# A 32×32 triangular inverse by columns in place, its steps spread over an RWKV-7 recurrence

## The chip, the core and the metric

The kernel runs on one core of one Trainium2 chip. A core has a matrix engine (TensorE, PE in the rows), three engines that work elementwise on SBUF (VectorE = DVE, ScalarE = ACT, GpSimd = POOL), a queue engine (SyncE = SP) that here issues most loads and stores, and 16 DMA engines. The metric is the device time of one execution in microseconds (us). [...]

## The reference

One inference step of a trunk of two mixing layers, each followed by a gated feed-forward layer: the first mixer is retention beside a gated linear recurrence, the second is RWKV-7. It runs over a prompt of 1024 tokens with 16 learned tokens ahead (1040 columns) and over 8 sample rows with states of their own. All is float32. The change lies in the RWKV-7 mixer:

```
def rwkv7_step(S, inp):
    r_t, w_t, k_t, v_t, a_t, b_t = inp
    sa = jnp.einsum('bhij,bhj->bhi', S, a_t)
    S = S * w_t[:, :, None, :] + sa[..., None] * b_t[:, :, None, :] + v_t[..., None] * k_t[:, :, None, :]
    y = jnp.einsum('bhij,bhj->bhi', S, r_t)
    return S, y
...
    s_new, ys = lax.scan(rwkv7_step, s0.astype(f32), (tm(rh), tm(wh), tm(kh), tm(vh), tm(-kk), tm(kk * ah)))
...
    o = ((ys - mu) * lax.rsqrt(var + GN_EPS_C)).reshape(B, T, D) * p['gn_g'].astype(f32) + p['gn_b'].astype(f32)
    bonus = jnp.sum(rh * kh * p['r_k'].astype(f32), axis=-1, keepdims=True) * vh
    o = (o + bonus.reshape(B, T, D)) * g.astype(f32)
    return o.astype(h.dtype) @ p['w_o'], s_new, h[:, -1], v_first
```

There are 16 heads of 64 channels. The kernel runs the prompt's scan in 17 chunks of 64 tokens (the last has 16). Within a chunk the step-by-step dependence becomes a triangular system (I − A) U = Z per head, with A strictly triangular; its solution takes the inverses of the two 32×32 diagonal blocks and one product for the block below them.

## The kernel before

The RWKV-7 mixer has two parts. `Layer1A` makes the projections r, k and v, each in eight output tiles of 128 features (two heads), over 1040 + 8 columns. A float32 product is three float32r passes on TensorE (`mm`, lines 335 to 337), after ScalarE and VectorE have split each operand in two (323, 324). Beside the products run *side steps*: the table POS gives each a place in sixths of a tile, and `weave` emits it between the eight parts of the tile's products. In the v stage these are, for each tile, the value transposes (`spread` and `tr`: VectorE adds the shift at 1385 and 1388, TensorE transposes at 1401 and 1404), the arithmetic of the 8 sample rows for one head pair (`samp_load`, `samp_pair`, `samp_sum`: loads on SyncE at 1509, elementwise work on VectorE and GpSimd at 1518 to 1530) and two entries of the inverse of block 0. After the last tile `samp_post` forms the sample rows' group norm (`sy` matmuls at 1542 and 1554 and small VectorE instructions at 1543 to 1558). When the tiles are done, `done()` issues the loads of chunk 0's keys (`load_k`), the side steps that are left follow in the order of their places, with `first`, which is `load_v` of chunk 0, among them.

The diagonal blocks are inverted four chunks at a time, one 32×32 block on a partition (4 chunks × 16 heads × 2 = 128 partitions; the fifth group has one chunk and 32 partitions). Such a group is called a block below. `inv_steps` returns a list of steps: `load` (GpSimd's queue: a DMA of the scores `d_ab` to the tile `at`, and memsets of the result `mt` to the unit matrix), `rows` between the given cuts (VectorE, one multiply and one sum for each row t from 1 to 31), and `out` (a transposed copy on VectorE, and two stores on GpSimd's queue to `d_mt` and `d_mm`, from which the chunks' loads on SyncE's queue read at 1680 and 1683).

`Layer1B` runs the recurrence: 17 chunks × 2 halves of the heads = 34 *units*. A unit's pieces are emitted in the order of the string UNIT; the engines run their own instructions in this order, each waiting only for its data. `pa`, `pt`, `p2`, `p3` prepare the next unit (scores `A`, transposes `Tp`, masks to `lz` and `ly` on VectorE), `z`, `u`, `s` and `y` are the chain (the state matmuls `s`, 16 of them, at 1796; the state's scaling on VectorE at 1804; its copies to `s0v` on GpSimd at 1812), `g1` and `g2` are the group norm of the unit before, `o` a part of the output projection of a block of tokens that is complete (from unit 8 on), and `r` takes one step from the list of the inverse, four times a unit. Block j is needed by chunk 4j; `run` makes its list at chunk 4(j − 1), 22 steps and an empty one long, so that in two of eight units the list is empty. Loads of chunk c + 2 are issued at the end of chunk c. 

```
CUTS = [1, 8, 11] + list(range(14, 33))
UNIT = "pa z pt g1 u r r o r p2 g2 o o s o r y p3"
```

Of the kernel before, what the change touches and what calls it, by code (L numbers as in the profile page):

```python
# [8 lines left out]
F32 = mybir.dt.float32  # L9
F32R = mybir.dt.float32r  # L10
AF = mybir.ActivationFunctionType
OP = mybir.AluOpType
# [3 lines left out]
T = 1048  # L16
# [10 lines left out]
NCH = 17  # L27
NTOK = 1040

# ---------------------------------------------------------------- vectors  # L30
# [14 lines left out]
def constants():  # L45
    """Tables that depend on shapes alone."""
# [41 lines left out]
# ---------------------------------------------------------------- host layout  # L88
def cols(v):
    """(..., n*128) -> (128, ..., n): features on partitions."""  # L90
    v = np.asarray(v)
    r = v.reshape(v.shape[:-1] + (v.shape[-1] // 128, 128))
    return np.moveaxis(r, -1, 0)


def wblocks(w):
    """(K, M) -> (M/128, 128, K/128 * 128): one block per 128 output features."""
# [4 lines left out]
def gblocks(w, groups):  # L102
    """(K, 1024) cut along K in groups of g tiles -> blocks that hold 8, 4 or 2 output tiles x g K-tiles."""
# [73 lines left out]
def unlayout(o):  # L177
# [15 lines left out]
# where the parts of a head pair's arithmetic stand beside the next products, in sixths of a 128-wide output tile  # L193
# [5 lines left out]
       0.69, "v.s2": 1.38, "v.sum": 4.97, "v7.pair": 2.3, "v7.post": 5.46, "v7.post_d": 0.5, "v.fold": 1.57, "v.tr0":  # L199
# [3 lines left out]
# K-tiles between stages of which GpSimd takes the lower part  # L203
POOL = (1, 3, 4)

# and of which it takes the mix
MIXP = (4,)

# shares of PE time given to the parts beside the products
L0K = {"start": 0.088, "rope": 0.5, "tr": 1.05, "ret0": 1.312, "ret": 0.35, "lru0": 2.42, "lru1": 2.2, "lru2": 2.2,  # L210
       "lru3": 1.76, "conv": 3.221, "group": 0.748, "wait": 3.6, "norm": 0.845, "norm1": 0.28}
# ---------------------------------------------------------------- device
# [4 lines left out]
class Weave:  # L217
    """Emits dense steps and, between them, side steps as their share of the time comes up."""
# [43 lines left out]
class Prog:  # L262
# [6 lines left out]
    # ---- weights: loads two blocks ahead, exact split into two float32r parts one block ahead  # L269
# [33 lines left out]
    def scale_w(self, t, kind, j):  # L303
        """Scales a block of w1 | a1 (or g1) by mix (j = 0) or 1 - mix along K."""
# [21 lines left out]
    # ---- one PSUM bank of a product: sum over k of W[k]^T X[k], in three exact float32r passes  # L326
# [21 lines left out]
    # steps of one 128-wide output tile, each token block in so many parts; evac(tb, psum view, c0, c1).  # L348
    # late: the weights of the next tile are not split before this one; pre: they are once its products are out
# [18 lines left out]
    # two tiles side by side at the start of a phase, each token block as soon as its norm is there  # L368
# [1716 lines left out]
```

## Time and profile before

| | |
|---|---|
| median of 3 runs | 3529.23 us (3525.82 to 3534.32) |
| profiled execution: span from first to last instruction | 3527.9 us |
| busy in the span: TensorE, VectorE, ScalarE, GpSimd | 94%, 51%, 35%, 10% |
| value stage, 2096 to 2204 us: TensorE, VectorE, GpSimd busy | 92.6, 92.7, 66.5 of 108.0 us |
| recurrence, 2231.4 to 2672.1 us: TensorE, VectorE, GpSimd busy | 366.3, 350.6, 85.6 of 440.7 us |
| granted clock over the whole span | 0.961 |

A row of the trace names an instruction by engine and line of the kernel, with out<-in by the program's names. The busy time of an engine counts its instructions, not its waits; a matmul's end is modelled. The bracket at the end of a row gives the idle time of the engine just before, and what ended it. The profiled execution's span is 1.3 us below the median of the runs. The stages in the middle of the span have different limits, so busy shares are read by stretch and not over the whole.

### The profile page before, as it was taken

How to read it: one execution, taken by the hardware profiler on the slowest of the kernel's cores; microseconds unless marked ns; L12 is line 12 of the kernel's file. 1: busy time of each engine (PE TensorE's matmuls, PEld its weight loads, DVE VectorE, ACT ScalarE, POOL GpSimd, SP SyncE). 2: the span in 40 equal slices, each digit the busy share in tenths (PEclk: the TensorE clock that was granted, in tenths of full speed). 3: DMA queues.
4: the chain of work that ended last, by engine and by line, in shares of the span. 5: the costliest groups of instructions: out<-in, count | busy, mean ns of one | idle time of the engine just before them, and what ended most of it. 6: DMA issues, size and time to landing. Idle time of an engine off the chain costs nothing.

```text
span 3527.9 us, 55814 instructions
## 1 busy us (share of the span) xinstructions
PE 3305.9 (94%) x23480; PEld 3123.5 (89%) x23480; DVE 1800.3 (51%) x2860; ACT 1241.4 (35%) x2214; POOL 361.6 (10%) x650
## 2 busy tenths in 40 slices
PE   8999999998999999998978978788889999999998
PEld 7999999997999999997978878566767999999997
DVE  4444445556433333334765658677885533333334
ACT  4222224555322212123674444344445312212122
POOL 0110110000000000000111236111210000000000
PEclk9999999999999999999999989678999999999999
DMA  4111211111111111111356768845543111111111
GB/s 134 62 56 60 74 40 46 46 47 34 42 43 48 48 48 42 42 53 48 118 169 169 176 172 232 219 119 143 152 129 96 37 49 46 45 49 42 48 48 64
DMA packets 303066, 294.33 MB, mean 83 GB/s; under 512 B 233056, under 2 KB 248704, under 8 KB 300640
## 3 DMA queue, kind: packets, MB, share of 16 engines
q1 hardware_dynamic: 294368, 262.95, 25.6%
q0 software_dynamic: 8448, 27.82, 2.5%
q8 instruction: 185, 3.03, 0.4%
q14 instruction: 65, 0.53, 0.1%
HBM read 218.95 MB, written 67.47 MB: 81 GB/s over the span
## 4 chain that ended last, share of the span: by engine, by line
PE 29%; DVE 12%; DMA 4%; ACT 3%; issue 3%; SPq 1%; POOL 1%; DVEq 0%; POOLq 0%; ACTq 0%
PE d L337 8%; PE d L335 8%; PE d L336 8%; DVE pr L1439 2%; DVE mt L1441 1%; PE hs L1325 1%; DVE xsl L324 1%; DMA x<-d_pp 1%; DVE wl L324 1%; DMA kq<-d_kq 1%; PE nrm L429 1%; DMA at<-d_ab 1%; DVE x L1213 1%; DVE T L1439 0%; ACT x L1188 0%
## 5 line engine op out<-in xcount | busy, mean ns | idle before, releaser
L335 PE MATMUL d<-xsh,wh 128*128 128x350 f32 (+1 forms) x3656 | 1207.6, 330 | 11.5 <-ACT xsh L323 7.7
L337 PE MATMUL d<-xsl,wh 128*128 128x350 f32 (+1 forms) x3656 | 1193.6, 326 | 5.2 <-DVE xsl L324 5.1
L336 PE MATMUL d<-xsh,wl 128*128 128x350 f32 (+1 forms) x3656 | 1188.0, 325 | 4.4 <-DVE wl L324 4.4
L335 PEld LDWEIGHTS d<-xsh,wh 128*128 128x128 f32 x3656 | 696.2, 190 | 23.2 <-ACT xsh L323 9.3
L337 PEld LDWEIGHTS d<-xsl,wh 128*128 128x128 f32 x3656 | 694.6, 190 | 16.0 <-DVE xsl L324 14.7
L336 PEld LDWEIGHTS d<-xsh,wl 128*128 128x128 f32 x3656 | 696.9, 191 | 7.1 <-DVE wl L324 5.2
L335 PE MATMUL d<-T,wh 128*128 128x350 f32 (+1 forms) x1380 | 463.7, 336 | 15.8 <-DVE x L405 8.9
L324 DVE TENSOR_TENSOR wl<-wst,wh 128x1024 fp32r<-128x1024 f32 x248 | 303.1, 1223 | 320.3 <-ACT wh L323 320.3
L336 PE MATMUL d<-T,wl 128*128 128x350 f32 (+1 forms) x1380 | 445.2, 323 | 2.5 <-DVE wl L324 2.5
L337 PE MATMUL d<-T,wh 128*128 128x350 f32 (+1 forms) x1380 | 445.3, 323 | 1.4 <-DVE T L324 1.4
L323 ACT ACTIVATE wh<-wst 128x1024 fp32r<-128x1024 f32 x248 | 260.7, 1051 | 509.2 <-PE d L337 387.8
L405 DVE TENSOR_TENSOR x<-d,x 128x350 f32<-128x350 f32 (+1 forms) x450 | 230.3, 520 | 322.2 <-PE d L337 322.1
L991 DVE SCALAR_TENSOR_TENSOR T<-T,vec 128x1064 f32<-128x1064 f32 x88 | 116.8, 1327 | 398.2 <-ACT T L989 396.6
L335 PEld LDWEIGHTS d<-T,wh 128*128 128x128 f32 x1380 | 260.0, 188 | 28.2 <-DVE x L405 10.2
L336 PEld LDWEIGHTS d<-T,wl 128*128 128x128 f32 x1380 | 260.1, 188 | 9.9 <-DVE wl L324 3.2
L337 PEld LDWEIGHTS d<-T,wh 128*128 128x128 f32 x1380 | 260.2, 189 | 2.2 <-DVE T L324 2.2
L323 ACT ACTIVATE T<-T 128x1048 fp32r<-128x1048 f32 (+2 forms) x77 | 69.2, 899 | 288.1 <-DVE T L1004 241.2
L985 POOL TENSOR_SCALAR fcout<-T 128x2 f32<-128x2 f32 x44 | 11.2, 254 | 1515.1 <-ACT T L983 1515.1
L983 ACT ACTIVATE T<-d 128x350 f32<-128x350 f32 (+1 forms) x88 | 40.5, 461 | 269.6 <-PE d L337 269.6
L324 DVE TENSOR_TENSOR T<-T 128x1048 fp32r<-128x1048 f32 (+2 forms) x77 | 78.9, 1024 | 76.7 <-ACT T L323 76.7
L1004 DVE TENSOR_TENSOR T<-T,d 128x350 f32<-128x350 f32 x88 | 45.2, 515 | 120.5 <-PE d L337 120.4
L1439 DVE TENSOR_TENSOR pr<-mt,at 128x1 f32<-128x1 f32 (+45 forms) x124 | 93.9, 757 | 19.1 <-DMA at<-d_ab 13.5
(412 smaller groups left out, 4261.4 us busy)
## 6 DMA issues: line engine op xcount, KB each, us to landing
wst<-in_w_up SPq DMA_DIRECT2D x88, 512.0 KB, 3.2
wst<-in_w_down SPq DMA_DIRECT2D x44, 512.0 KB, 3.6
wst<-in_w_in SPq DMA_DIRECT2D x40, 512.0 KB, 3.2
kq<-d_kq SPq DMA_DIRECT2D x17, 1024.0 KB, 6.7
wst<-in_w_o SPq DMA_DIRECT2D x32, 512.0 KB, 4.0
T<-d_sv SPq DMA_DIRECT2D x80, 128.0 KB, 3.8
d_kq<-x SPq DMA_DIRECT2D x16, 544.0 KB, 4.4
d_kq<-x SPq DMA_DIRECT2D x32, 272.0 KB, 5.4
```

The costliest lines, as they stand in the source:

```text
L323: self.nc.scalar.activation(out=h, in_=src, func=AF.Copy)
L324: (eng or self.nc.vector).tensor_tensor(out=l, in0=src, in1=h.bitcast(F32), op=OP.subtract)
L335: mm(ps, lhsT=h, rhs=a, start=start and j == 0, stop=False)
L336: mm(ps, lhsT=l, rhs=a, start=False, stop=False)
L337: mm(ps, lhsT=h, rhs=b, start=False, stop=stop and j == n - 1)
L405: self.nc.vector.tensor_tensor(out=xv, in0=ps, in1=xv, op=OP.add)
L429: self.nc.tensor.matmul(self.nps[tb][:, :n], lhsT=self.ones, rhs=sq, start=m == 0, stop=m == 7)
L983: nc.scalar.activation(out=ub[:, 18 + c0:18 + c1], in_=ps, func=AF.Copy)
L991: nc.vector.scalar_tensor_tensor(out=c, in0=ub[:, j:1064 + j], scalar=w[j], in1=c, op0=OP.mult, op1=OP.add)
L1004: nc.vector.tensor_tensor(out=st["f"][:, c0:c1], in0=c[:, 16 + c0:16 + c1], in1=ps, op=OP.mult)
L1213: nc.vector.tensor_tensor_scan(L, self.rst, s, 0.0, OP.mult, OP.add)
L1439: nc.vector.tensor_tensor(out=pr, in0=mt[:, 0:t, 0:t], in1=at[:, 0:t, t].unsqueeze(1).to_broadcast([n, t, t]), op=OP.mult)
```

## The change

Three things change.

- The inverse of a block is built in place and by columns. The scores are loaded straight into `mt`, the diagonal is set to 1 after the load has landed, and for each s from 1 to 30 VectorE multiplies column s above the diagonal by row s right of it (an outer product of s × (31 − s) elements, at most 240) and adds it to the rectangle above and to the right. The row form had t × t elements for t up to 31 and a sum over them. `pr` shrinks to 240 columns and is doubled, `mt` is doubled, the transposed copy gets a tile `tt` of its own.
- Its steps are spread. Block 0's list in the v stage has 14 entries and ends in tile 7, behind the last sample pair (it had 11 and ended in tile 6). In the recurrence the four blocks form one list of 113 entries, taken by four a unit from unit 0 on: block 1 in 19 parts, blocks 2 to 4 one column (two instructions) at a time. The load of a block is issued together with the `out` of the block before it, ahead of that one's stores.
- The last steps of the sample rows (`samp_post`, the `sy` matmuls and what follows) move from 5.46 to 8.2 sixths, behind the transposes of the last value tile.

Comments and docstrings are dropped too, without effect. Lines shift by one: 1439 to 1440, 1441 to 1442, 1796 to 1797, 1804 to 1805.

```diff
-       0.69, "v.s2": 1.38, "v.sum": 4.97, "v7.pair": 2.3, "v7.post": 5.46, "v7.post_d": 0.5, "v.fold": 1.57, "v.tr0":
+       0.69, "v.s2": 1.38, "v.sum": 4.97, "v7.pair": 2.3, "v7.post": 8.2, "v7.post_d": 0.01, "v.fold": 1.57, "v.tr0":
...
         def load():
-            at = st["at"] = alloc("at")[:n, 0:1024]
-            nc.gpsimd.dma_start(out=at, in_=flat(d["ab"][4 * j:min(4 * j + 4, NCH)]))
             mt = st["mt"] = alloc("mt")[:n, 0:1024]
-            nc.gpsimd.memset(mt, 0.0)
+            nc.gpsimd.dma_start(out=mt, in_=flat(d["ab"][4 * j:min(4 * j + 4, NCH)]))
             nc.gpsimd.memset(mt[:, 0:1024:33], 1.0)
 
-        def rows(t0, t1):
-            at, mt = (st[k].rearrange("p (a b) -> p a b", b=32) for k in ("at", "mt"))
-            for t in range(t0, t1):
-                pr = alloc("pr")[:n, :t * t].rearrange("p (c s) -> p c s", s=t)
-                nc.vector.tensor_tensor(out=pr, in0=mt[:, 0:t, 0:t],
-                                        in1=at[:, 0:t, t].unsqueeze(1).to_broadcast([n, t, t]), op=OP.mult)
-                nc.vector.tensor_reduce(mt[:, 0:t, t], pr, mybir.AxisListType.X, OP.add)
+        def cols(s0, s1):
+            mt = st["mt"].rearrange("p (a b) -> p a b", b=32)
+            for s in range(s0, s1):
+                k = 31 - s
+                pr = alloc("pr")[:n, :s * k].rearrange("p (c t) -> p c t", t=k)
+                nc.vector.tensor_tensor(out=pr, in0=mt[:, 0:s, s].unsqueeze(2).to_broadcast([n, s, k]),
+                                        in1=mt[:, s, s + 1:32].unsqueeze(1).to_broadcast([n, s, k]), op=OP.mult)
+                nc.vector.tensor_tensor(out=mt[:, 0:s, s + 1:32], in0=mt[:, 0:s, s + 1:32], in1=pr, op=OP.add)
...
-            tt = alloc("pr")[:n, 0:1024]
+            tt = alloc("tt")[:n, 0:1024]
...
-        inv = self.inv_steps(0, dict(zip(("at", "mt", "pr"), (B[4], B[6], B[7]))).get,
-                             [1, 8, 13, 17, 20, 23, 26, 28, 30, 32])
+        inv = self.inv_steps(0, dict(zip(("mt", "pr", "tt"), (B[6], B[7][:, 0:240], B[4]))).get,
+                             [1, 6, 9, 11, 13, 15, 17, 19, 21, 23, 26, 31], 1)
...
-CUTS = [1, 8, 11] + list(range(14, 33))
+CUTS = [[1, 4] + list(range(8, 24)) + [26, 31]] + [list(range(1, 32))] * 3
...
-        alloc = lambda tag: self.ivp.tile([128, 1024], F32, tag=tag, name=tag)
+        alloc = lambda tag: self.ivp.tile([128, 240 if tag == "pr" else 1024], F32, tag=tag, name=tag,
+                                          bufs=1 if tag == "tt" else 2)
...
         inv = []
+        for j, cuts in enumerate(CUTS):
+            s = self.a.inv_steps(j + 1, alloc, cuts)
+            if j:
+                last, ahead = inv.pop(), s[0]
+                inv.append(lambda last=last, ahead=ahead: (ahead(), last()))
+            else:
+                s[0]()
+            inv += s[1:]
         out = []
         for i, u in enumerate(units):
             c, f = u
-            if c % 4 == 0 and f == 0 and c // 4 + 1 < 5:
-                inv = self.a.inv_steps(c // 4 + 1, alloc, CUTS, 1)
```

How the engines' own order moves is seen at three places. On VectorE in the recurrence, before, from the state's scaling of unit 3 to the end of the first block's rows in unit 4 (`pr` and `mt` are the inverse, `lz` and `ly` the masked scores, `yf` the group norm):

```order
L1804 TENSOR_TENSOR S<-S,scl 128x256
L1439 TENSOR_TENSOR pr<-mt,at 128x784
L1441 TENSOR_REDUCE mt<-pr 128x28
L1718 TENSOR_TENSOR lz<-A,masks 64x4x64 x2
L1721 TENSOR_TENSOR ly<-A,masks 128x256 x2
L1846 SCALAR_TENSOR_TENSOR yf<-y,yf 128x256
L1439 TENSOR_TENSOR pr<-mt,at 128x841
L1441 TENSOR_REDUCE mt<-pr 128x29
L1439 TENSOR_TENSOR pr<-mt,at 128x900
L1441 TENSOR_REDUCE mt<-pr 128x30
L1439 TENSOR_TENSOR pr<-mt,at 128x961
L1441 TENSOR_REDUCE mt<-pr 128x31
```

and after, the same stretch of the unit at the columns with the most elements:

```order
L1805 TENSOR_TENSOR S<-S,scl 128x256
L1440 TENSOR_TENSOR pr<-mt 128x238
L1442 TENSOR_TENSOR mt<-mt,pr 128x17x14
L1719 TENSOR_TENSOR lz<-A,masks 64x4x64 x2
L1722 TENSOR_TENSOR ly<-A,masks 128x256 x2
L1847 SCALAR_TENSOR_TENSOR yf<-y,yf 128x256
L1440 TENSOR_TENSOR pr<-mt 128x234
L1442 TENSOR_TENSOR mt<-mt,pr 128x18x13
L1440 TENSOR_TENSOR pr<-mt 128x228
L1442 TENSOR_TENSOR mt<-mt,pr 128x19x12
L1440 TENSOR_TENSOR pr<-mt 128x220
L1442 TENSOR_TENSOR mt<-mt,pr 128x20x11
```

The places in the unit are the same; each step has a multiply and an add of a quarter of the elements. On GpSimd at the end of the v stage, before, the products of sample pair 6 (`T`) with the stores of block 0 behind them, and further on the first memsets of the recurrence's tiles:

```order
L1526 TENSOR_TENSOR T<-T 128x512
L1448 DMA d_mt<-x 128x1024
L1449 DMA d_mm<-T 128x1024
L1193 MEMSET x 128x48 x2
L1506 DMA T<-in_st_rwkv 128x512
```

and after, behind the products of pair 7:

```order
L1527 TENSOR_TENSOR T<-T 128x512
L1526 DMA out_rwkv_s<-T 128x512
L1193 MEMSET T 128x48 x2
L1449 DMA d_mt<-x 128x1024
L1450 DMA d_mm<-x 128x1024
L1678 MEMSET s0v 64x8x64
L1685 MEMSET mt 32x8x32
```

The two stores have moved from between pairs 6 and 7 to behind both. On TensorE at the same place, before (`d` are the products of the last v tile, `hp` its low-rank part, `vt` the value transposes, `A` the first scores of the recurrence):

```order
L1542 MATMUL sy<-T,masks 128x64
L335 MATMUL d<-xsh,wh 128x348
L336 MATMUL d<-xsh,wl 128x348
L337 MATMUL d<-xsl,wh 128x348
L1343 MATMUL hp<-masks,tmp 128x128 x3
L335 MATMUL d<-xsh,wh 128x348
L336 MATMUL d<-xsh,wl 128x348
L337 MATMUL d<-xsl,wh 128x348
L1554 MATMUL sy_18741<-T,masks 128x64
L1343 MATMUL hp<-masks,tmp 128x128 x3
L1401 MATMUL vt<-masks,T 128x128 x8
```

and after:

```order
L1343 MATMUL hp<-masks,tmp 128x128 x3
L1401 MATMUL vt<-masks,T 128x128 x8
L1343 MATMUL hp<-masks,tmp 128x128 x3
L1404 MATMUL vt<-masks,T 64x128
L1543 MATMUL sy<-T,masks 128x64
L1555 MATMUL sy_18776<-T,masks 128x64
L1710 MATMUL A<-kq 128x128 x8
```

The two `sy` matmuls now stand behind the last transposes, right ahead of the recurrence's first scores.

## Rows read from the trace of the kernel before

**Rows 1.** Page: busy tenths in 40 equal slices of the span.
```profile
PE   8999999998999999998978978788889999999998
...
DVE  4444445556433333334765658677885533333334
```

**Rows 2.** One stretch, matmuls of line 1796 alone (columns as in rows 3).
```profile
2448.80:2539.70 90.90, 4.97 (x96) 4.04 (x96) 0.87 0.49 132
```

**Rows 3.** Stretches: us, then busy of PE, PEld, DVE, ACT, POOL; clock, DMA share, GB/s.
```profile
2231.40:2270.00 38.60, 30.76 (x426) 23.49 (x420) 27.52 (x73) 15.52 (x46) 7.38 (x10) 0.69 0.93 267
2270.00:2312.90 42.90, 33.45 (x422) 24.83 (x421) 38.61 (x60) 16.69 (x50) 10.08 (x12) 0.61 0.35 95
2312.90:2333.50 20.60, 19.35 (x281) 14.80 (x280) 10.38 (x26) 10.74 (x31) 4.41 (x7) 0.74 0.65 169
2333.50:2353.60 20.10, 11.74 (x160) 9.46 (x159) 11.59 (x40) 6.91 (x20) 3.12 (x5) 0.83 0.50 90
...
2353.60:2672.10 318.50, 270.99 (x3775) 223.45 (x3774) 262.51 (x509) 151.18 (x393) 60.57 (x80) 0.90 0.50 137
2353.60:2427.30 73.70, 60.76 (x821) 50.03 (x820) 66.70 (x113) 33.65 (x89) 13.29 (x18) 0.88 0.49 137
...
2427.30:2448.80 21.50, 21.50 (x331) 17.83 (x330) 13.06 (x30) 12.70 (x33) 5.63 (x9) 1.00 0.69 196
2448.80:2539.70 90.90, 73.24 (x985) 60.18 (x984) 78.66 (x154) 39.78 (x105) 16.40 (x20) 0.87 0.49 132
```

**Rows 4.** Costly lines of VectorE, 2231.4 to 2672.1 us: busy, mean ns | idle before.
```profile
L1439 DVE TENSOR_TENSOR pr<-mt,at 128x1 f32<-128x1 f32 (+45 forms) x124 | 93.9, 757 | 19.1 <-DMA at<-d_ab 13.5 <-POOL mt L1433 3.3
L1441 DVE TENSOR_REDUCE mt<-pr 128x1 f32<-128x1 f32 (+45 forms) x124 | 62.2, 502 | 4.3
```

**Rows 5.** Timeline, single VectorE instructions of the recurrence: start us, duration us.
```profile
2235.76 0.26 DVE L1439 TENSOR_TENSOR pr<-mt,at 128x64 f32<-128x64 f32 x1
2236.05 0.22 DVE L1441 TENSOR_REDUCE mt<-pr 128x8 f32<-128x64 f32 x1
...
2301.53 1.81 DVE L1439 TENSOR_TENSOR pr<-mt,at 128x961 f32<-128x961 f32 x1
2303.38 1.16 DVE L1441 TENSOR_REDUCE mt<-pr 128x31 f32<-128x961 f32 x1
...
2308.32 1.05 DVE L1446 COPY pr<-mt 128x1024 f32<-128x1024 f32 x1
...
2555.09 0.42 DVE L1804 TENSOR_TENSOR S<-S,scl 128x256 f32<-128x256 f32 x1
```

**Rows 6.** The chain that ended last, 2150 to 2420 us: start, us, what.
```profile
2211.18 7.60 DMA kq<-d_kq
...
2333.03 7.34 DMA at<-d_ab
```

**Rows 7.** Costly lines of VectorE in the value stage, 2096 to 2177 us.
```profile
L1439 DVE TENSOR_TENSOR T<-x 128x1 f32<-128x1 f32 (+30 forms) x31 | 32.5, 1047 | 8.2 <-DMA x<-d_ab 7.4
L1441 DVE TENSOR_REDUCE x<-T 128x1 f32<-128x1 f32 (+30 forms) x31 | 15.7, 505 | 1.1
```

**Rows 8.** The value stage as one stretch (columns as in rows 3).
```profile
2096.00:2204.00 108.00, 92.64 (x571) 88.77 (x570) 92.71 (x120) 43.75 (x96) 66.49 (x60) 0.95 0.87 232
```

**Rows 9.** Timeline at the end of the value stage: VectorE, GpSimd, SyncE's queue.
```profile
2188.71 0.58 POOL L1448 DMA_DIRECT2D d_mt<-x  x1
...
2207.80 1.28 DVE L1530 TENSOR_REDUCE T<-T 128x8 f32<-128x512 f32 x2
...
2214.44 1.20 SPq L1680 DMA_DIRECT2D mt<-d_mt  x2
```

**Rows 10.** DMA issue of the value stage: size, median us to landing.
```profile
d_mm<-T POOLq DMA_DIRECT2D x1, 512.0 KB, 6.2
```

**Rows 11.** Timeline in the value stage: GpSimd beside VectorE.
```profile
2108.84 2.09 POOL L1523 TENSOR_TENSOR T<-T,smp_v 128x512 f32<-128x512 f32 x1
...
2109.95 1.11 DVE L1439 TENSOR_TENSOR T<-x 128x64 f32<-128x64 f32 x1
```

More of the change, by code (lines that the diff above doesn't have):

```diff
@@ L1449, in out @@
             nc.gpsimd.dma_start(out=flat(d["mm"][4 * j:min(4 * j + 4, NCH)]), in_=tt)
-        return [load] + [lambda: None] * wait + [lambda a=a, b=b: rows(a, b) for a, b in zip(cuts[:-1], cuts[1:])] + [out]
+        return [load] + [lambda: None] * wait + [lambda a=a, b=b: cols(a, b) for a, b in zip(cuts[:-1], cuts[1:])] + [out]
     def samp_pre(self):
```

## Prediction

> **What bounds the kernel now.** I read the page's slices first, then a table of the recurrence by stretches, then the costly lines and single instructions of the engine that stands out. The slices [rows 1] show TensorE at 9 tenths nearly everywhere. In slices 25 to 30 (88.2 us each, so 2117 to 2646 us), the value stage of RWKV-7 and its recurrence, it stands at 7 and 8 while VectorE's row stands at 6 to 8, its densest stretch. Only there does the change act. The span is 3527.9 us and the median of the runs 3529.2, so what I take off the span I take off the median.
>
> The recurrence has 17 chunks of two units each. I cut its time at the state matmuls of a unit, 16 of them each time: 96 in a row are six units [rows 2]. In [rows 3] the rows are, one after the other, units 0–2, 3–5, 6–7, 8, then 9–31 together, and of these 9–13, 14–15 and 16–21. In units 14–15 the list of inverse steps is empty: TensorE is busy 21.50 of 21.50 us, VectorE 13.06, the granted clock 1.00. In 16–21, which carry inverse steps, TensorE is busy 73.24 of 90.90 us at 0.87 and VectorE 78.66. So a unit without inverse is TensorE's, 10.75 us long, and one with it is VectorE's, 14.7 to 15.2. The VectorE time beyond 6.5 us a unit (13.06 / 2) is the inverse, [rows 4]: 93.9 us in multiplies and 62.2 in sums, four blocks, 39.0 us each. VectorE itself is idle 1.4 us (73.70 − 66.70 over five) to 2.0 us (90.90 − 78.66 over six) in such a unit; I keep these as its unavoidable waits.
>
> **The inverse's new price.** Before, 31 rows with t·t elements make 62 instructions and twice 10,416 elements. [Rows 5] split an instruction into a start and a slope: the sum takes 0.22 us at 64 and 1.16 at 961, so 1.05 ns an element and 0.15 us fixed; the multiply 0.26 and 1.81, so 1.73 ns and 0.15. That gives 38.3 us a block against 39.0 measured. After, 30 columns with s(31−s) elements are 60 instructions and twice 4,960 elements. What a multiply costs that repeats an element along the inner direction, the trace shows in the state's scaling L1804: 256 elements in 0.42 us, so 1.05 ns. At this price a block is 60 × 0.153 + 9,920 × 1.05 ns = 19.6 us. If the new multiply kept the 1.73 of the old one it is 22.9. I take 19.6: L1804 has the same form of operand, while the old multiply walked down a column, a new place of stride 32 for each element. [...]
>
> **Units 9 to 31** (318.5 us for 23, 13.85 each [rows 3]). The new list has one column pair per slot, four slots a unit, with no empty stretch before unit 28. VectorE then needs 6.5 + 4 × 2 × 0.34 = 9.2 us on average (0.34 with the gap between two instructions), 9.8 where a column has 240 elements; with its 1.4 to 2.0 us of waits 10.6 to 11.8. TensorE's floor is 10.75. The two nearly meet, and I take 10.9 us: 250.7, a gain of **68**. At the floor of 10.75 it is 71; at 11.8 in every unit 47. What is late next is TensorE itself, at the full clock. The wait that can remain is local: of the four pairs two or three stand ahead of the mask products and the group norm's subtraction in VectorE's row, and units 14–15 have no slack on TensorE.
>
> **Units 3 to 8** (42.90 + 20.60 + 20.10 = 83.6). The largest rows of the first block and a 7.34 us wait for the next block's load [rows 6] lie here; the load now goes out ahead of the previous block's end, with the slots of a unit between. No output projection runs yet, and the clock is at 0.61 to 0.83. I take units 3–7 as the present empty pair, 20.6 / 2 = 10.3, and unit 8 as 10.75: 62.3, a gain of **21**. If the clock stays cold, units 3–7 need TensorE's 33.45 / 3 = 11.15: gain 17. If they run as light as VectorE allows (10.38 / 2 = 5.2 of other work, 2.4 for small columns, 1.4 of waits: 9.0), gain 28.
>
> **The value stage and units 0 to 2.** Block 0 costs VectorE 48 us there [rows 7] and should cost 20 to 28. But VectorE is not alone: in 2096–2204 [rows 8] TensorE is idle 15.4 of 108 us, and the DMA engines are busy 0.87, so that at most 14 us could go. The sample rows' loads and sums set much of it, and they stay. Of the gain I take 8. On the other side stands the end of block 0. It was written at 2188.7 [rows 9]; now its last five pairs and the copy stand behind sample pair 7 on VectorE, whose sums end at 2209, so the two stores leave GpSimd at about 2213 (five pairs of 0.6, a copy of 1.05 [rows 5]) and the later one lands 6.2 us after that [rows 10], at about 2219. SyncE reaches its read of them at 2214.44 [rows 9]. It waits some 4 us there, and behind it queue the rest of the first chunk's loads, the last value stores, the loads of s0v and uv and the next chunk. Net **+4**, ends −4 and +10. The samples' last matmuls and small VectorE instructions that move behind the value transposes I cost at nothing: TensorE waits 7.60 us for the first chunk's load right there [rows 6]; without that cover they are some 3 us more on the path. The new wait of the diagonal's memset for its block's load holds GpSimd for the time of a load, up to the 7.34 us of [rows 6], four times, and behind it the stores of the block before and copies of the state. The copy is needed a unit later, some 10 us, which covers it; without that cover it is 4 × 7 = 28 us at most.
>
> **The sum:** 68 + 21 + 4 = 93; 3529 − 93 = **3436 us**. The ends together: 71 + 28 + 10 = 109, 3420; and 47 + 17 − 4 = 60, 3469.
>
> **Rivals.** *VectorE keeps the recurrence* (chance 0.17). Multiplies at 1.73 add 3.3 us a block, 0.4 a unit, and the waits stay at 2.0: 9.2 + 0.4 + 2.0 = 11.6, a gain of 52, with 17 and 4: 73, **3456**. For it: in no stretch with inverse steps was VectorE idle less than 1.4 us. Against: L1804.
>
> *The head stays bound by loads* (0.13). SyncE's wait at the first read of the inverse is not hidden, so the early chunks come 5 us later, and units 3–7 stay cold: 68 + 17 − 5 = 80, **3449**. For it: the DMA share 0.93 in units 0–2 [rows 3].
>
> *All hidden costs come out at nothing* (0.05): the floor everywhere, **3420**.
>
> *Slower: the adds take what the sums gave back* (0.03). The old sum reads one operand, the new add two. In the value stage a multiply of 64 elements took 1.11 us with a GpSimd product beside it [rows 11] and 0.26 without [rows 5]; its mean was 1047 ns there [rows 7] against 757 [rows 4], while the sum had 505 and 502. If every one of the 60 instructions of a block met this 0.85 us, a block would cost 19.6 + 51 = 71 us, 9.4 a unit, and a unit 6.5 + 9.4 + 2 = 17.9: 23 of them 412 against 318.5, 93 more, 76 when the head's 17 is taken off, **3605**. It decides from about 0.46 us on every instruction (48 us a block, 6.4 a unit, 14.9 with the rest and the waits, which eats the head's gain too). Against it: GpSimd is busy 13.29 of 73.70 us in units 9–13 (18%), 66.49 of 108 in the value stage (62%). [...]
>
> That the change doesn't spread the steps is excluded by the rows of the order above.
>
> **Chances.** Forecast 0.62, its own range 3424 to 3452; the rivals 0.17, 0.13, 0.05 and 0.03. The range is 3413 to 3474: the ends of the sum, widened by the spread of the runs before (3525.8 to 3534.3). It leaves out the slower case and little more. Two runs of this kernel can be told apart from about 0.2%, 7 us. Faster 0.96, within that 0.01, slower 0.03.
>
> **What would show it.** Units 9–31: TensorE busy over 95% at a clock of 0.97 or more, about 10.9 us between two groups of state matmuls; if they are 11.5 or more with VectorE idle under 1 us, the first rival holds. The multiplies and adds of a block: mean 0.32 us each; 0.4 or more for the multiply alone speaks for the column price, 0.7 for both for the slower case. The block-0 stores at 2213 and a wait of SyncE at the read of the inverse; if the store comes before 2205 I have its place wrong. If the stretch from 2096 to 2270 shrinks by over 15 us, the value stage was VectorE's and I have it too small; if the gain is under 50 us with both engines idle in the recurrence, the loads or GpSimd's waits have taken over.

## Result and the profile after

| | median, us | ratio to before (95%) |
|---|---|---|
| before | 3527.53 (3524.24 to 3534.32, 4 runs) | |
| changed | 3446.76 (3443.60 to 3453.52, 4 runs) | 0.9767 (0.9749 to 0.9786) |

The change took 80.8 us off, where 93 were forecast. The profiled execution of the changed kernel has a span of 3445.2 us, 82.7 less than that of before. The recurrence by stretches, cut at the state matmuls as in [rows 3] (us, then busy time of PE, PEld, DVE, ACT, POOL; mean granted clock, with 1.00 for full speed; DMA share, GB/s). The rows are units 0–2, 3–5, 6–7, 8, all of 9–31, and of these 14–15 and 16–21:

```profile
2228.50:2267.50 39.00, 29.60 (x426) 22.62 (x421) 23.99 (x65) 15.39 (x46) 5.81 (x8) 0.70 0.93 263
2267.50:2301.50 34.00, 27.82 (x421) 20.99 (x420) 26.24 (x76) 16.33 (x48) 8.78 (x14) 0.80 0.59 160
2301.50:2321.60 20.10, 15.87 (x281) 11.79 (x280) 16.35 (x43) 11.32 (x35) 4.07 (x6) 0.97 0.58 141
2321.60:2335.00 13.40, 13.40 (x161) 10.99 (x160) 9.70 (x24) 7.56 (x20) 1.69 (x2) 0.67 0.33 83
2335.00:2587.30 252.30, 246.92 (x3773) 204.13 (x3772) 200.35 (x492) 151.71 (x391) 51.74 (x78) 1.00 0.66 174
2389.40:2411.90 22.50, 21.61 (x331) 17.82 (x330) 19.34 (x47) 13.16 (x35) 4.02 (x6) 1.00 0.65 166
2411.90:2478.20 66.30, 64.29 (x985) 53.11 (x984) 54.46 (x138) 39.49 (x103) 14.01 (x22) 1.00 0.69 183
```

Against [rows 3], units 9–31 went from 318.5 to 252.3 us (10.97 a unit), with TensorE busy 246.92 us at a clock of 1.00; VectorE lost 62 us of work (262.51 to 200.35). Units 16–21, which were VectorE's, went from 90.9 to 66.3. Units 14–15, which had no inverse and were 21.5, are now 22.5: the work that was missing there has come in. Units 3–8 went from 83.6 to 67.5, units 0–2 from 38.6 to 39.0, and unit 0 begins 2.9 us earlier. Together 66.2 + 16.1 − 0.4 + 2.9 = 84.8 us. Some 2 us less arrive at the end of the span, most of them behind a product near the end of the last feed-forward layer: from there to the end it is 103.4 us before and 105.0 after. Over all profiles of this document it is 103.3 to 103.4 in eight, of kernels with rows and with columns, and 104.8 to 105.0 in six, so the columns do not set it.

The costly lines of VectorE in the recurrence (busy us, mean ns | idle before it), the answer to [rows 4], and then the same lines in the value stage, the answer to [rows 7]:

```profile
L1442 DVE TENSOR_TENSOR mt<-mt,pr 128x58 f32<-128x58 f32 (+29 forms) x119 | 40.5, 340 | 4.4
L1440 DVE TENSOR_TENSOR pr<-mt 128x84 f32<-128x84 f32 (+29 forms) x118 | 39.8, 338 | 5.8 <-DMA mt<-d_ab 4.3
...
L1440 DVE TENSOR_TENSOR T<-x 128x30 f32<-128x30 f32 (+14 forms) x30 | 18.1, 604 | 0.7
L1442 DVE TENSOR_TENSOR x<-x,T 128x30 f32<-128x30 f32 (+14 forms) x30 | 14.4, 480 | 1.0
```

A block costs (40.5 + 39.8) / 4 = 20.1 us instead of 39.0; 19.6 was the estimate. Multiply and add cost the same. What TensorE waited for, first before (2353.6 to 2650 us), then after (2335 to 2544 us; from there to the end of unit 31 the view shows no wait): in total, times, longest. `Tp` are transposes of the unit's preparation, `y` at 1856 (after: 1857) is the second matmul of the group norm.

```profile
PE Tp L1733 <- ACT mt L1760: 24.2, 13, 4.7
PE y L1856 <- ACT sq L1848: 23.3, 13, 2.9
```

```profile
PE y L1857 <- ACT sq L1849: 5.0, 13, 0.6
```

These 47.5 us of waits became 5.0. Both waits of before go through ScalarE. At the group norm ScalarE itself waited for VectorE's subtraction (`sq` on `yf`, 53.7 us in this stretch), which stands behind a row of the inverse.

### The profile page after: what moved, and what is told of

Read it like the earlier page. It is cut to its first block, busy times and chain, and to the rows that moved or that the text cites. A ratio compares the mean times of both kernels' runs of the same rounds, so it can differ in the third digit from the quotient of the medians.

```text
span 3445.2 us, 55808 instructions
## 1 busy us (share of the span) xinstructions
PE 3272.4 (95%) x23480; PEld 3098.2 (90%) x23480; DVE 1709.7 (50%) x2850; ACT 1242.1 (36%) x2214; POOL 336.9 (10%) x645
## 4 chain that ended last, share of the span: by engine, by line
PE 32%; DVE 8%; ACT 4%; DMA 3%; issue 2%; SPq 2%; POOL 0%; DVEq 0%; ACTq 0%; POOLq 0%
PE d L335 9%; PE d L337 9%; PE d L336 9%; PE hs L1325 1%; DMA kq<-d_kq 1%; DVE xsl L324 1%; ACT wh L323 1%; DMA x<-d_pp 1%; PE A L1710 1%; PE nrm L429 1%; DVE x L1213 1%; DVE lz L1719 1%; DMA d_vt<-x 0%; SPq L1510 0%; PE y L1827 0%
## 5 line engine op out<-in xcount | busy, mean ns | idle before, releaser
L337 PEld LDWEIGHTS d<-xsl,wh 128*128 128x128 f32 x3656 | 694.7, 190 | 16.6 <-DVE xsl L324 15.8
L985 POOL TENSOR_SCALAR fcout<-T 128x2 f32<-128x2 f32 x44 | 11.2, 254 | 1515.3 <-ACT T L983 1515.3
L983 ACT ACTIVATE T<-d 128x350 f32<-128x350 f32 (+1 forms) x88 | 40.5, 462 | 269.6 <-PE d L337 269.6
L429 PE MATMUL nrm<-tmp,ones 128*128 128x350 f32 (+1 forms) x208 | 77.8, 479 | 15.4 <-ACT tmp L419 14.9
```

Source lines behind the costliest of these rows:

```text
L337: mm(ps, lhsT=h, rhs=b, start=False, stop=stop and j == n - 1)
L429: self.nc.tensor.matmul(self.nps[tb][:, :n], lhsT=self.ones, rhs=sq, start=m == 0, stop=m == 7)
L983: nc.scalar.activation(out=ub[:, 18 + c0:18 + c1], in_=ps, func=AF.Copy)
```

## Experiments

Chips and stages differ a little from run to run, also ahead of the change (one product early in the value stage began between 2076 and 2093 us in the profiles). So times are compared as ratios to before on the same chip, and stages by their own length. The ratio of the changed kernel is 0.9767, and 0.9758 in a second set of runs below; 0.001 is 3.5 us.

### Price or spread: columns at the old places

```diff
-CUTS = [[1, 4] + list(range(8, 24)) + [26, 31]] + [list(range(1, 32))] * 3
+CUTS = [1, 3, 5, 6, 8, 9] + list(range(10, 21)) + [22, 24, 26, 28, 31]
...
+            if c % 4 == 0 and f == 0 and c // 4 + 1 < 5:
+                inv = self.a.inv_steps(c // 4 + 1, alloc, CUTS, 1)
```

> Blocks 1 to 4 in the new column form, but at the places of before: a list of 21 parts and an empty step, begun at every fourth chunk, so that two of eight units carry no inverse. Block 0 and the sample rows as in the changed kernel (3446.8 us). Theory (the price of a block is what was gained, the even spread adds little): VectorE needs 6.5 + 3.7 us in five to six of eight units, with 1.5 us of waits 11.7, and 10.75 in the rest: some 8 to 12 us over the changed kernel, 3455 to 3459. Rival (the spread carries half of the gain or more): 3485 or more, with units of 13 us.

Measured: 0.9832 (0.9816 to 0.9847), 23 us over the changed kernel. By its ratio it lies between the theory and the rival. Units 9–31 took 269.5 us. Three stretches, units 8, 16 and 20, and what VectorE waited for in units 8 to 31:

```profile
2321.20:2339.70 18.50, 12.69 (x159) 10.22 (x158) 10.54 (x30) 8.20 (x23) 1.97 (x4) 0.82 0.48 94
2420.40:2437.60 17.20, 13.70 (x167) 11.41 (x166) 11.43 (x32) 7.46 (x20) 1.93 (x3) 0.80 0.43 116
2470.20:2483.90 13.70, 11.73 (x165) 9.71 (x164) 12.56 (x32) 7.38 (x20) 1.93 (x2) 0.92 0.37 108
...
DVE pr L1440 <- DMA mt<-d_ab: 13.8, 3, 7.6
```

In units 8 and 16 VectorE stands idle for 8.0 of 18.5 us and 5.8 of 17.2: the block's first multiply waits for a load that was sent only two slots ahead, and all that stands behind it on VectorE waits too. Unit 20 has late parts of a block, two columns in one slot; there TensorE waits 1.9 us at the group norm. So the columns alone gave 59 us of the 82, and the list's shape 23. Against the changed kernel units 8, 16 and 24, the first of a block, are 12.7 us longer together, and units 12, 20 and 28, with thick parts, 10.1; the others together are 0.5 shorter. So the shape pays by sending the load ahead and by leaving no thick parts.

### Price or spread: rows, spread

```diff
+        by_rows = j > 0
...
-CUTS = [[1, 4] + list(range(8, 24)) + [26, 31]] + [list(range(1, 32))] * 3
+CUTS = [[1, 4] + list(range(8, 24)) + [26, 32]] + [[1, 3] + list(range(4, 33))] * 3
...
-                inv.append(lambda last=last, ahead=ahead: (ahead(), last()))
+                inv.append(lambda last=last, ahead=ahead: (last(), ahead()))
```

> Blocks 1 to 4 in the old row form (a multiply and a sum for each row), but spread as in the changed kernel, one row per slot; block 0 and the sample rows as in the changed kernel. Theory: VectorE pays 39 us a block wherever it stands; small rows hide behind TensorE's 10.75 us, the units with rows 22 to 31 last 14 to 18: about 105 us per eight units against 112 before and 88 now, so 3490 to 3510. Rival (the spread carries half of the gain or more): 3485 or less.

Measured: 1.0000 (0.9987 to 1.0014), no gain at all, and neither number was met. One unit (unit 4, the thick last part of block 1), and the multiplies of the inverse:

```profile
2274.10:2304.60 30.50, 12.68 (x141) 9.47 (x140) 27.59 (x33) 5.88 (x19) 3.95 (x5) 0.50 0.14 39
...
L1455 DVE TENSOR_TENSOR pr<-mt,at 128x1 f32<-128x1 f32 (+45 forms) x124 | 93.7, 756 | 30.6 <-DMA at<-d_ab 28.9
```

VectorE waited 28.9 us for loads, since with single tiles a block's load cannot go out before the block ahead is done; and six of the largest rows in one slot made a unit of 30.5 us at a clock of 0.50. The run did not answer its question, so it was made again without these two faults (against the run before, not the changed kernel):

```diff
-CUTS = [[1, 4] + list(range(8, 24)) + [26, 32]] + [[1, 3] + list(range(4, 33))] * 3
+CUTS = [[1, 8, 11] + list(range(14, 28)) + [28, 29, 30, 31, 32]] + [[1, 3] + list(range(4, 33))] * 3
...
-        alloc = lambda tag: self.ivp.tile([128, 1024], F32, tag=tag, name=tag)
+        alloc = lambda tag: self.ivp.tile([128, 1024], F32, tag=tag, name=tag, bufs=1 if tag == "pr" else 2)
...
-                last, ahead = inv.pop(), s[0]
-                inv.append(lambda last=last, ahead=ahead: (last(), ahead()))
+                g, ahead = inv[-5], s[0]
+                inv[-5] = lambda g=g, ahead=ahead: (g(), ahead())
```

> As the run with rows spread (row form in blocks 1 to 4, one row per slot), but with the scores' and the result's tiles doubled, each block's load sent four slots before the block ahead of it ends, and block 1 cut into even parts. Theory (there the 28.9 us in which VectorE waited for the loads and the 30 us unit at the end of block 1 hid what the even spread gives the row form): 15 to 35 us under before, ratio 0.990 to 0.996; large rows still make units of 14 to 18 us. Rival (VectorE's 39 us a block eat the spread's gain also without these waits): within 0.002 of before.

Measured: 0.9955 (0.9937 to 0.9973), 16 us under before, at the near end of what the theory had. Units 9–31, and the multiplies:

```profile
2348.20:2650.50 302.30, 263.71 (x3775) 217.87 (x3774) 256.82 (x501) 150.25 (x391) 60.09 (x80) 0.93 0.54 145
...
L1455 DVE TENSOR_TENSOR pr<-mt,at 128x1 f32<-128x1 f32 (+45 forms) x124 | 93.7, 755 | 24.6 <-DMA d_mm<-pr 12.7 <-DMA at<-d_ab 10.3
```

302 us instead of 318.5: spreading alone cannot take out VectorE's 257 us of work, and a single transposed copy still makes it wait (12.7 us for the store of `d_mm`). Price alone 59, spread alone 16, both 82: the two parts add up with little over. Both runs have the changed kernel's value stage; by units 0–31 alone, where it does not count, the three are 61.6, 16.6 and 81.9 us under before.

### What the columns still cost: without them

```diff
-            for s in range(s0, s1):
+            for s in range(s0, s1) if j == 0 else []:
```

> The changed kernel without the multiplies and adds of blocks 1 to 4 (this part of the computation is left out; loads, diagonal, copies and stores of the blocks stay): the price of what is left of the inverse in the recurrence. Theory (TensorE bounds units 9 to 31 at 10.65 to 10.75 us and the columns cost only local waits): units 9 to 31 take 246 us against 252.3, units 3 to 8 some 3 us less, so 8 to 12 us under the changed kernel. Rival (VectorE still sets the pace in many units): 20 us or more under.

Measured: 0.9735 (0.9711 to 0.9758), 8 to 11 us under the changed kernel by its two ratios, as expected. Units 3–8 and 9–31:

```profile
2258.20:2318.20 60.00, 54.25 (x861) 42.05 (x860) 32.43 (x80) 33.86 (x97) 14.41 (x22) 0.87 0.59 156
2318.20:2563.80 245.60, 245.60 (x3773) 204.07 (x3772) 157.57 (x349) 153.87 (x393) 51.68 (x78) 1.00 0.66 178
```

TensorE is busy in every one of the 245.60 us. So of units 9–31's 252.3 us only 6.7 are owed to the columns, and TensorE is the bound there. In units 3–8 the columns still cost 7.5 us; 3 were expected. This kernel leaves out a part of the computation.

### How near VectorE is: each multiply twice

```diff
+                for _ in range(2 if j > 0 else 1):
                     nc.vector.tensor_tensor(out=pr, in0=mt[:, 0:s, s].unsqueeze(2).to_broadcast([n, s, k]),
```

> The changed kernel with every multiply of blocks 1 to 4 issued twice: 120 more VectorE instructions of 0.34 us, 40 us in all, 1.3 to 1.7 us in each of some 28 units. Theory (VectorE's 8.7 us and its 1.5 us of waits nearly meet TensorE's 10.75): a unit gets 11.6 to 11.9 us long, 15 to 22 us over the changed kernel. Rival 1 (TensorE bounds with room to spare): under 8 us. Rival 2 (VectorE bounds each unit already): 32 to 40 us.

Measured: 0.9830 (0.9809 to 0.9851), 22 to 25 us over. The multiplies, and units 9–31:

```profile
L1441 DVE TENSOR_TENSOR pr<-mt 128x30 f32<-128x30 f32 (+29 forms) x240 | 81.1, 338 | 12.8 <-DMA mt<-d_ab 4.0 <-DMA d_gg<-T 3.1
...
2341.60:2606.60 265.00, 248.33 (x3773) 205.40 (x3772) 224.23 (x565) 151.61 (x393) 52.13 (x78) 0.99 0.62 165
```

Of 41 us more on VectorE half came through, 12.7 of them in units 9–31: VectorE is no longer the bound, but it is the next one, with little slack. The theory holds; its upper end was a little low.

### The local wait: the fourth slot moved, then the load sent further ahead

```diff
-UNIT = "pa z pt g1 u r r o r p2 g2 o o s o r y p3"
+UNIT = "pa z pt g1 u r r o r r p2 g2 o o s o y p3"
```

> The changed kernel with a unit's fourth inverse slot moved from behind the state's scaling to behind the third slot, so that on VectorE all four pairs stand behind the mask products and the group norm's subtraction. Theory (the columns cost what TensorE waits at the group norm's second matmul, 0.3 to 0.6 us in 13 units shown and some spread behind it): 4 to 7 us under the changed kernel, units 14 to 17 at 10.8 us. Rival (the wait only moves to another of VectorE's products): within 2 us of it.

Measured: 0.9766 (0.9742 to 0.9790), no change; the forecast of 4 to 7 us failed. What TensorE waited for in units 13 to 19, then units 6–7, 8 and 12 as stretches, and one of the waits in unit 12:

```profile
PE y L1857 <- ACT sq L1849: 0.6, 3, 0.2
...
2293.40:2311.30 17.90, 15.29 (x281) 11.56 (x280) 15.63 (x42) 10.79 (x32) 3.99 (x6) 1.00 0.53 137
2311.30:2322.00 10.70, 10.03 (x159) 8.19 (x158) 9.09 (x24) 6.87 (x20) 1.69 (x2) 1.00 0.49 113
...
2354.80:2370.40 15.60, 13.78 (x166) 11.57 (x165) 11.26 (x29) 7.85 (x21) 2.93 (x5) 0.78 0.76 209
...
DVE pr L1440 <- DMA mt<-d_ab: 2.1, 1, 2.1
```

The wait at the group norm's second matmul fell from 2.7 to 0.6 us in these units, and units 14 to 17 took 10.7 to 11.2 us. Units 6–8 gained most: 28.6 us instead of 33.5, at a clock of 1.00. But unit 12 lasted 15.6 us and unit 20 12.2, where both were 10.9: with the slots together, the first column of the next block comes before its load has landed. The load was then sent four slots earlier:

```diff
-                last, ahead = inv.pop(), s[0]
-                inv.append(lambda last=last, ahead=ahead: (ahead(), last()))
+                g, ahead = inv[-5], s[0]
+                inv[-5] = lambda g=g, ahead=ahead: (g(), ahead())
```

> The changed kernel with the fourth inverse slot behind the third, as in the run with early slots, and each block's load sent four slots before the end of the block ahead of it. Theory (the early slots took TensorE's wait at the group norm away, and units 12 and 20 gave it back, 15.6 and 12.2 us, because the next block's first column waited for its load): units 12 and 20 at 10.8 us, units 9 to 31 at 247 to 249 us, 3 to 6 us under the changed kernel. Rival (something else made units 12 and 20 long): no change against the run with early slots.

The changed kernel ran again beside it:

> The changed kernel once more, beside the next three on the same chip. Expected: a ratio to before of 0.975 to 0.979; in the trace units 9 to 31 at 252 us and units 3 to 8 at 67 us, as in its first profile.

Measured: 0.9758 (0.9741 to 0.9775) for the changed kernel, 252.4 us in units 9–31 and 67.4 in units 3–8; 0.9742 (0.9726 to 0.9759) with early slots and early loads. Its units 9–31, and TensorE's wait between 2324.8 and 2544 us:

```profile
2324.80:2574.40 249.60, 246.94 (x3775) 204.11 (x3774) 199.55 (x493) 150.95 (x393) 51.60 (x78) 1.00 0.66 175
...
PE y L1857 <- ACT sq L1849: 1.8, 8, 0.3
```

Unit 12 was 10.78 us and unit 20 10.66, as the theory had them. 249.6 us is 2.8 less than the changed kernel and 0.6 more than forecast; units 3–8 took 63.9, 3.5 less, with unit 8 again at 10.7 us. The time, 6 us less by the ratios, has an interval that overlaps the other's.

### The clock in units 3 to 8: filler matmuls

```diff
+        fill = p.bank()
...
+                    elif op == "o" and 3 <= i < 8:
+                        for _ in range(2):
+                            nc.tensor.matmul(fill[:, 0:128], lhsT=p.ones, rhs=p.ones, start=True, stop=True)
```

> The changed kernel with two matmuls on constants (128 x 128, result unused) at each output slot of units 3 to 7, where TensorE has gaps and no output projection runs. Theory (units 5 and 8 are 11.4 and 13.3 us long because the granted clock falls to half behind units with gaps): the clock of unit 8 rises from 0.67 to over 0.9, 2 to 5 us under the changed kernel. Rival (the filler takes as much as it gives, or the clock falls nevertheless): 0 to 4 us over.

Measured: 0.9762 (0.9740 to 0.9784), which can't be told from the changed kernel. In the profile the clock did what was expected; units 3–7, then unit 8:

```profile
2274.90:2327.00 52.10, 46.95 (x770) 37.70 (x769) 40.87 (x113) 26.41 (x78) 12.88 (x20) 1.00 0.58 156
2327.00:2338.30 11.30, 10.05 (x161) 8.16 (x160) 9.14 (x24) 6.83 (x19) 1.69 (x2) 1.00 0.54 112
```

At a clock of 1.00 unit 8 took 11.3 us instead of 13.4, and units 3–8 63.4 instead of 67.5. These 4.1 us came back with the clock; units 0–2 and 9–31 of this profile were 1.5 us longer each, so the sum stayed within the measurement. The early slots had the clock at 1.00 in units 6–8 without a filler, and units 3–8 at 62.4 us: with TensorE idle 2.6 of 17.9 us in units 6–7, where it was 4.2 of 20.1, the clock did not fall.

### The head: sample rows back, block 0 back

```diff
...
-"v7.post": 8.2, "v7.post_d": 0.01
+"v7.post": 5.46, "v7.post_d": 0.5
...
```

> The changed kernel with the last steps of the sample rows back at 5.46 sixths, ahead of the value transposes. Theory (the loads of the first chunk bound the head, these steps are hidden at either place): within 3 us of the changed kernel, 3444 to 3450. Rival (the second sum now stands behind block 0's tail on VectorE until 2205 us, and TensorE waits for it ahead of the transposes): 4 to 6 us more, 3451 to 3453.

Measured: 0.9760 (0.9743 to 0.9777), the same as the changed kernel. TensorE's wait ahead of the last value transposes, in the changed kernel and then here:

```profile
2205.49 1.97 PE L1401 MATMUL vt<-masks,T 128*128 128x128 f32 x8 [6.38 <-DVE x L1385]
```

```profile
2204.13 0.66 PE L1543 MATMUL sy<-T,masks 128*128 128x64 f32 x2 [5.91 <-DVE T L1531]
```

It waits some 6 us at either place, for VectorE. In the changed kernel VectorE is at the last sample pair until 2200.6 us, and then for 3.8 us at the last five column pairs and the copy of block 0, which the change has put there. The move of the sample steps is worth nothing that could be measured.

```diff
...
-        inv = self.inv_steps(0, dict(zip(("mt", "pr", "tt"), (B[6], B[7][:, 0:240], B[4]))).get,
-                             [1, 6, 9, 11, 13, 15, 17, 19, 21, 23, 26, 31], 1)
+        inv = self.inv_steps(0, dict(zip(("at", "mt", "pr"), (B[4], B[6], B[7]))).get,
+                             [1, 8, 13, 17, 20, 23, 26, 28, 30, 32])
```

> The changed kernel with block 0 as before: row form, 11 entries, ended in tile 6. The recurrence and the sample rows as in the changed kernel. Theory (the DMA engines bound the end of the value stage and the first loads, so that what VectorE saves in block 0 is given back there): 0 to 4 us over the changed kernel, 3447 to 3451, with the last value tile some 8 us later and the first scores of the recurrence 0 to 4 us later. Rival (VectorE bounds the value stage): 8 to 10 us over, 3455 to 3457.

Measured: 0.9777 (0.9757 to 0.9798), 4 to 7 us over the changed kernel by its two ratios, between the theory and the rival; the interval takes in both ratios, so no difference is shown. From one product early in the value stage (the 3501st matmul on line 335) to a product of the last value tile (the 3651st) it took 105.1 us, as before (104.9), against 95.8 and 97.2 in the two profiles of the changed kernel; from the first of these products to unit 0's state matmuls it is 144.4 us against 140.1 and 143.2 (142.2 before). The 8 to 9 us that VectorE gives back by the last tile shrink to 1 to 4 within the next 45 us. Eight more profiles of this document have the changed kernel's value stage and sample steps; over all ten, the way to unit 0 takes 139.9 to 143.2 us, 142.0 in the mean. Against the 142.2 of before, no gain at unit 0 is shown.

Where they go: SyncE's queue, and GpSimd's, in the changed kernel (the answer to [rows 9]), the first chunk's load (size, median us from the start of its issue to landing; it was 7.6 before), and the stretch from the last value tile to unit 0, after and then before:

```profile
2199.92 0.69 DVE L1531 TENSOR_REDUCE T<-T 128x8 f32<-128x512 f32 x1
...
2203.59 0.89 POOL L1449 DMA_DIRECT2D d_mt<-x  x1 [3.34 <-DVE x L1442]
...
2204.59 5.28 SPq L1671 DMA_DIRECT2D kq<-d_kq  x1
2209.97 0.55 SPq L1676 DMA_DIRECT2D lz<-d_kq  x1
2210.62 1.08 SPq L1681 DMA_DIRECT2D mt<-d_mt  x2
...
kq<-d_kq SPq DMA_DIRECT2D x2, 1024.0 KB, 11.3
...
2184.00:2230.00 46.00, 28.51 (x245) 25.07 (x243) 24.37 (x59) 15.14 (x38) 13.83 (x20) 0.72 0.96 241
```

```profile
2194.00:2232.00 38.00, 27.84 (x232) 24.41 (x231) 21.89 (x39) 14.79 (x37) 13.27 (x18) 0.72 0.94 239
```

SyncE reaches the first chunk's load 6.6 us earlier than before (2211.18, [rows 6]), but the load lands only 2.9 us earlier: the DMA engines are busy 0.96 of the time at 241 GB/s, as before. In SyncE's queue the issue itself takes 5.28 us here, 2.52 before, and 0.3 to 0.4 from the third chunk on. Values, states, a weight block and now block 0's two stores are under way at the same time; that they are what delays the load is argued from the DMA share, as no run takes them away. In this profile SyncE does not wait at its read of `d_mt`. In the second profile of the same kernel the issue takes 2.62 us, the stores leave at 2205.5, the load lands 12.5 us after the start of its issue, and SyncE waits at both reads of block 0:

```profile
SPq L1681 <- DMA d_mt<-x: 1.6, 1, 1.6
SPq L1684 <- DMA d_mm<-x: 1.2, 1, 1.2
```

So it is in nine of the twelve profiles in which block 0 ends in tile 7, with 2.8 to 6.5 us. Where it is 5.8 or more (five profiles), unit 0 comes 13.1 to 14.4 us behind the first scores, and 12.5 to 12.8 in the other seven: the long wait goes with some 1 us at unit 0.

### The head: the residual's load moved

```diff
-        for c0, c1 in TBS:
-            nc.sync.dma_start(out=p.x[:, :, c0:c1], in_=self.d["x"][:, :, c0:c1])
...
+            if i in (3, 4, 5):
+                c0, c1 = TBS[i - 3]
+                nc.sync.dma_start(out=p.x[:, :, c0:c1], in_=self.d["x"][:, :, c0:c1])
```

This stands on top of the early slots and early loads.

> The run before it, and the three loads of the residual x (4.3 MB on SyncE's queue, issued ahead of unit 0) moved to the ends of units 3, 4 and 5, where the DMA share is lower. Theory (the loads of chunks 1 and 2 wait behind x on the DMA engines, which are busy 0.93 of units 0 to 2): units 0 to 2 some 4 to 8 us shorter, units 3 to 8 at most 3 us longer, so 2 to 6 us less than the run before it. Rival (the bytes only move, and the gap shows up in units 3 to 6): within 2 us of it.

Measured: 3429.07 us (3418.46 to 3436.29), 0.9722 (0.9701 to 0.9743), against 0.9758 for the changed kernel and 0.9742 without this edit on the same chip. Units 0–2 and 3–8:

```profile
2235.30:2266.70 31.40, 29.14 (x424) 22.42 (x420) 24.16 (x67) 15.35 (x45) 6.29 (x9) 0.75 0.81 198
2266.70:2329.20 62.50, 53.74 (x861) 41.01 (x860) 51.13 (x140) 34.36 (x100) 13.60 (x21) 0.89 0.77 214
```

Units 0–2 took 31.4 us instead of 40.6 in the run before it, more than was forecast, and units 3–8 were not longer (62.5 against 63.9): the bytes found room. But unit 0 of this profile began 4.9 us later behind the product early in the value stage (146.6 us against 141.7), which the moved loads do not explain, as SyncE had issued them at 2231.7, behind unit 0's start. From that product to unit 9 it is 240.4 us against 246.2, 5.8 less, and the intervals of the two runs overlap, so this step by itself is not shown. This version is the fastest here, 13 us (0.36%) under the changed kernel by the medians and by the ratios; the intervals just touch.

## Why the prediction was right, and where it was off

The forecast was 3436 with a range of 3413 to 3474; the time is 3446.8, inside, on the slow side, and inside the forecast's own 3424 to 3452. It is also 2 us from the 3449 of the second rival, so it is the stages and not the number that tell them apart. The terms 68, 21 and 4 came out as 66.2, 16.1 and 2.5 in the first profile, and as 66.1, 16.2 and −0.4 in the second.

*The price of a block.* Right: 20.1 us measured against 19.6, multiply and add 338 and 340 ns against 0.32 us. Price alone gave 61.6 of the 81.9 us in units 0–31. The column price of 1.73 ns an element is gone. A pair with 240 elements shows it, at 0.41 us for each (0.15 + 240 × 1.05 ns = 0.40):

```profile
2410.09 0.41 DVE L1440 TENSOR_TENSOR pr<-mt 128x240 f32<-128x240 f32 x1
2410.54 0.41 DVE L1442 TENSOR_TENSOR mt<-mt,pr 128x240 f32<-128x240 f32 x1
```

That the old multiply's walk with a stride of 32 cost it the 1.73 is the author's estimate, as no run changes the stride alone.

*Units 9 to 31.* Right: gain 66.2 against 68, 10.97 us a unit against 10.9, TensorE busy 98% at a clock of 1.00 where over 95% and 0.97 had been named. What is late next is TensorE, and the run without columns shows its 245.6 us as the floor. The local wait of the mask products and the group norm behind the pairs is there, at 5.0 us in all.

*Units 3 to 8.* The mechanism was right, the size off: 16.1 instead of 21. The mis-sized term is that units 3–7 were taken at 10.3 us and unit 8 at 10.75. Units 3–7 took 10.8 each, and unit 8 took 13.4 at a mean clock of 0.67 (0.50 from 2321.6 to 2330 us, 1.00 from 2332), right behind units 6 and 7, in which TensorE was busy 15.87 of 20.1 us. What was left out is the local wait, which the prediction had named for units 9–31 and put at nothing here; in units 3–8 it is longer than in all of units 9–31:

```profile
PE y L1857 <- ACT sq L1849: 6.0, 4, 1.6
```

With the early slots units 6–7 took 17.9 us and unit 8 10.7, the value taken, at a clock of 1.00. The lower end of 17, the case of the low clock, was the better value.

*The value stage.* The net of +4 is not shown: unit 0 begins 2.9 us earlier in the first profile and 0.1 in the second, and over ten profiles the way to it is as long as before. Its first part is there at the last value tile, 7.7 to 9.1 us where 8 were taken. The loss was put at a wait of SyncE behind stores at 2213. The stores left at 2203.6 (2205.5 in the second profile), since sample pair 7 itself ended at 2200.6 and not 2209; a store before 2205 is the sign that the prediction had named for a wrong place. The wait of SyncE at its read is absent in the first profile and 2.8 us in the second, and where it is longest it goes with some 1 us at unit 0. Most of the loss is ahead of it: from the product early in the value stage to the first scores it is 127.4 and 130.3 us against 129.6 before. The first chunk's load, which does not read the inverse, lands 11.3 and 12.5 us after the start of its issue instead of 7.6, with the DMA engines at 0.96 and 0.97. That the bytes under way do this is not shown by a run of its own.

The samples' last steps were rightly put at nothing (the run with them moved back), but the cover was misread: the 7.60 us of [rows 6] are the load's time from its issue, and TensorE's wait ahead of the first scores was 1.20 us before:

```profile
2218.82 1.01 PE L1709 MATMUL A<-kq 64*128 64x128 f32 x6 [1.20 <-DMA kq<-d_kq]
```

*GpSimd's new wait.* It sat idle 18.3 us ahead of the four memsets of the recurrence (line 1433, engine idle until, us and times), and nobody waited for it, as costed:

```profile
  DMA mt<-d_ab: 18.3, 4
```

*The rivals.* VectorE did not keep the recurrence: units are 10.97 us and not 11.6. The second rival's gain of 17 in units 3–8 is what came (16.1), and its wait of SyncE is there in most profiles, but the early chunks do not come 5 us later and units 9–31 are as in the forecast. The slower case did not come, but what it counts on is there: beside a copy on GpSimd a multiply of 234 elements took 0.48 us where one of 240 took 0.41, and in the value stage, with GpSimd busy 64.3 of the 120 us from 2085 to 2205, the two-input add has a mean of 480 ns against 340 in the recurrence, while the old sum had 505 and 502.

```profile
2406.34 1.80 POOL L1813 TENSOR_SCALAR s0v<-S 64x256 f32<-64x256 f32 x2 [9.38 <-DVE S L1805]
2406.51 0.48 DVE L1440 TENSOR_TENSOR pr<-mt 128x234 f32<-128x234 f32 x1
```

Why it takes longer there is not shown. In the recurrence 34 multiplies and adds lie wholly within a copy of 0.84 us and are 0.08 us longer in the mean than others of their shape, 0.24 at most. With GpSimd busy 51.74 of the 252.3 us of units 9–31, the price is small: 34 × 0.08 = 2.7 us.

## What to carry to other kernels

When two engines alternate as the bound, count the time of each in the stretches where the other is idle: here VectorE's 39 us a block became 20, and the gain stopped where TensorE's own floor began (252.3 us against 245.6 without the columns). An even list of small steps is worth little by itself; it pays because the next load can go out ahead and no thick step stands in front of what others wait for. Look at each short stretch for a local wait of TensorE: here the clock was 0.67 in the unit behind one, and one slot moved behind VectorE's work for the group norm brought back 4.9 us in three units. Work that was saved where the DMA engines were at 0.96 did not show at the next stage, so there bytes that can go later are worth a try.

## What was not expected

The list's shape gave 23 us on top of the columns, more than half of it at block boundaries: 7.6 us of VectorE idle for one load made a unit of 18.5 us. Both kernels read 4.3 MB of residual in units 0 to 2, though the output projection begins in unit 8; without it those units were 9 us shorter, and the time 5 to 7 us by medians and ratios, within overlapping intervals.
